# The first projection in two halves of 272 columns, copied unscaled, with idle transposes ahead: a two-block model on one core

## The chip, the core and the metric

The program runs on one core of one Trainium2 chip. The metric is the device time of one execution in microseconds, as the median of the runs. The core has five engines that each run their own list of instructions in order: TensorE (PE, matmuls; its weight loads are shown as PEld), VectorE (DVE), ScalarE (ACT), GpSimd (POOL) and SyncE (SP, which only issues DMA here).

## What is computed

Two blocks follow each other on 256 rows of 1024 numbers, in float32. The first block has a latent attention (MLA) and a differential attention side by side, a gated merge, and a mixture of 16 experts; the second has convolution, stick-breaking attention and gating, a feed-forward part and a gated projection. The change touches the very beginning, the latent attention's inputs:

```python
h = _rms_norm(x, attn_norm_w)
z = jnp.einsum('btd,dc->btc', h, w_in)
c_q, c_kv, k_rope, dq, dk, dv, g_mla, g_diff = _split_columns(z)      # 256, 256, 32, ...
q = jnp.einsum('btr,rc->btc', _rms_norm(c_q, mla_q_norm_w), mla_w_uq).reshape(b, t, 16, 96)
kv = jnp.einsum('btr,rc->btc', _rms_norm(c_kv, mla_kv_norm_w), mla_w_ukv).reshape(b, t, 16, 128)
k_nope, v_mla = kv[..., :64], kv[..., 64:]
```

The first 544 columns of `z` are `c_q`, `c_kv` and `k_rope`. The RMS norm of `x` multiplies each row by a factor (called rx below), and the norms of `c_q` and `c_kv` by two more (rc).

## The kernel before

The kernel is written on a scheduling layer. TensorE and GpSimd keep the order in which the code is written; ScalarE and VectorE are ordered by a static scheduler, except inside the block `with self.tc.manual_schedule(...)` of `mla` (L597 to L621), where they too keep the written order. DMA issues on SP are placed by the scheduler.

Products keep float32 accuracy by splitting each operand into a high and a low part: `mm3` (L207) issues three matmuls, high x high (L209), low x high (L210) and high x low (L211). A weight piece is split by `put` (L118): ScalarE casts the high part `wh` (L120), VectorE subtracts to get the low part `wl` (L121). `feed`, `take` and `look` (L123 to L139) hand the pieces out in order and split `ahead` + 1 of them early. Three pairs of `wh`, `wl` buffers go round; weight tiles arrive in a ring of four slots, and a slot is loaded again when its pieces are split. `transpose_split` (L147) transposes 128 columns of both row tiles on TensorE into one PSUM bank, ScalarE writes the high part and VectorE the low part of the scaled result.

The beginning of `mla` (L584) runs so. `x` arrives in two halves of 512 columns. TensorE transposes the four chunks of the first half, then of the second (L599, L603), into the banks `tr`, `o`, `tr`, `mm`. The 544 columns of `w_in` come as four tiles of two chunks of 128 rows each, 128 x 1088 numbers; `step` runs, for each of the eight chunks, the products into four banks (two row tiles, two column halves of 272), 96 in all. In between stand the tables of the rotary embedding (`tables`, L449): GpSimd computes the angles from the positions, ScalarE takes the sine (L483) and loads the table of the exponential (L484), GpSimd also fills the distances for the second attention (L480, L481). The row factor rx is made by `rms` on VectorE: squares (L535, L537) and then twelve small steps of an inverse root (`rsqrt`, L81). The four banks are copied to `cc` scaled by rx (`scaled`, L619), `cc` is transposed in four chunks (L626), the row factor rc of its two parts is made (L627 to L631), and `up` (L638) runs the second step: 36 products of 512 columns for q (L662, copied unscaled by `put_q`) and 48 for k and v (L692), whose results `put_kv` scales by rc on the way out of their banks: VectorE copies row tile 0, ScalarE row tile 1 (L659, L660). These groups of products take turns in three banks (`mm`, `mm`, `su`). The row sums of q's squares (L674, L675) are made meanwhile. The scratch tile `cn` for the squares of `cc` and the tile `di` of the distances share the memory `d1`.

After that come the remaining columns of `w_in`, the two attentions, the merge and the router. Then the expert weights, 403 MB, stream in from SP; their first slots come free as the pools of this front stage are closed.

Of the kernel before, what the change touches and what calls it, by code (L numbers as in the profile page):

```python
# [13 lines left out]
F32 = mybir.dt.float32  # L14
F32R = mybir.dt.float32r
I32 = mybir.dt.int32
# [58 lines left out]
class Kernel:  # L75
# [373 lines left out]
    def tables(self):  # L449
# [4 lines left out]
        pos_r = fp.tile([128, T], I32, name="pos_r")  # L454
        nc.sync.dma_start(pos_r, A["positions"].to_broadcast((128, T)))
# [20 lines left out]
        g.tensor_scalar(ang, ang, PI_IN, -PI_IN, op0=ALU.min, op1=ALU.max)  # L476
        di = fp.tile([128, NT, T], I32, name="di", tag="d1")
# [4 lines left out]
        yield  # L482
        nc.scalar.activation(rope, ang, AF.Sin)  # L483
        nc.scalar.activation(self.warm, self.warm, AF.Exp)  # L484
        yield
# [9 lines left out]
        for j in range(2):  # L495
            for i, (wi, si) in enumerate(((0, 1), (1, 0), (0, 0), (1, 1))):
                for t in range(NT):
                    g.tensor_tensor(
                        self.tab[:, j, i, t, :], rope[:, si, t, :], wr[:, j, 16 * wi : 16 * wi + 16], op=ALU.mult
                    )  # L500

    def lam(self):

        nc, A, fp, cp, c = self.nc, self.A, self.fp, self.cp, self.col
        lr = self.lr
# [15 lines left out]
        lp = fp.tile([128, 2, 64], F32, name="lp")  # L521
        ls = fp.tile([128, 2], F32, name="ls")
        nc.vector.tensor_tensor(lp, lr[:, 0::2, :], lr[:, 1::2, :], op=ALU.mult)
        nc.vector.tensor_reduce(ls, lp, axis=AX.X, op=ALU.add)
        nc.scalar.activation(ls, ls, AF.Exp)
        self.nlam = fp.tile([128, 1], F32, name="nlam")

        nc.vector.scalar_tensor_tensor(self.nlam, ls[:, 1:2], -0.2, ls[:, 0:1], op0=ALU.add, op1=ALU.subtract)
# [12 lines left out]
    def front_tiles(self):  # L541
# [4 lines left out]
        for k0 in (0, 2, 4, 6):  # L546
            yield self.wload(W[:, k0 : k0 + 2, 0:544], 2, 544)
# [36 lines left out]
    def mla(self, fb):  # L584
# [3 lines left out]
        put = lambda cs: self.transpose_split(self.x, self.col["attn_norm_w"], xh, xl, cs, ("tr", "o", "tr", "mm"))  # L588

        def step(k, wh, wl):  # L590
            for t in range(NT):
                ts = slice(t * 128, t * 128 + 128)
                for h in range(2):
                    hs = slice(272 * h, 272 * h + 272)
                    self.mm3(pss[t][h][:, :272], xh[:, k, ts], xl[:, k, ts], wh[:, hs], wl[:, hs], k == 0, k == 7)

        with self.tc.manual_schedule(engines={mybir.EngineType.Activation, mybir.EngineType.DVE}):  # L597
            next(self.const)
            put(range(4))  # L599
# [3 lines left out]
            put(range(4, 8))  # L603
            self.ahead = 1
            ws = []
            tables = self.tables()
            for k in range(8):
                ws = ws or self.take()
                step(k, *ws.pop(0))
                if k == 2:  # L610
                    next(tables)
                if k == 6:
                    next(tables)
                if k == 4:
                    self.rx = rx = self.rms(self.fa, self.x, self.od)
            cc = fb.tile([128, NT, 544], F32, name="cc", tag="d0")
            for h in range(2):
                for t in range(NT):
                    self.scaled(cc[:, t, 272 * h : 272 * h + 272], pss[t][h][:, :272], rx[:, t : t + 1], t == 0)  # L619
# [3 lines left out]
        cn = fb.tile([128, NT, 512], F32, name="cn", tag="d1")  # L623
        ch = fb.tile([128, 2, 4, T], F32R, name="ch", tag="d2")
        h, l = ch[:, 0], ch[:, 1]
# [1101 lines left out]
```

## Time and profile before

| | us |
|---|---|
| median of 3 runs (1518.96 to 1519.03) | 1519.02 |
| the profiled execution | 1517.97 |
| its span, from the first to the last event | 1516.3 |
| TensorE busy in the span | 1151.3 |
| VectorE busy | 478.4 |
| ScalarE busy | 356.8 |
| GpSimd busy | 133.2 |

Rows that are quoted below come from the profiled execution and are in microseconds from the start of its span. A timeline row names the start, the duration, the engine, the line of the kernel, the operation, the tile it writes and those it reads, its shape and how many were merged (x2); in brackets stands how long the engine was idle before it, and what ended that. Durations of neighbours overlap a little, since an engine starts an instruction before the last one's end is through. A stretch row gives the busy time of each engine between two moments, the number of instructions, and the TensorE clock that was granted as a share of the full one (1.00 is 2.4 GHz, 0.50 is 1.2 GHz); the column also prints 1.00 where no level was recorded, as in the first 14 us.

### The profile page before, as it was taken

What the parts mean: (1) busy time and instruction counts of PE and PEld (TensorE: products, weight loads), DVE (VectorE), ACT (ScalarE), POOL (GpSimd) and SP (SyncE); (2) the same over time, 40 slices, a digit from 0 to 9 for tenths busy, and PEclk for the clock granted to TensorE, in tenths of its full rate; (3) what the DMA queues carried; (4) which work ended last, traced back from release to release, by engine and by line L of the source; (5) the groups of instructions that cost most, each with busy time, mean ns of one, the idle gap of its engine ahead of it and who ended that gap; (6) DMA issues with size and microseconds to landing.
All of it is one profiled execution on the core that took longest, in us unless ns stands there. A gap on an engine that the chain in (4) does not pass through costs nothing.

```text
span 1516.3 us, 16564 instructions
## 1 busy us (share of the span) xinstructions
PE 1151.3 (76%) x6795; PEld 632.2 (42%) x6795; DVE 478.4 (32%) x969; ACT 356.8 (24%) x644; POOL 133.2 (9%) x181
## 2 busy tenths in 40 slices
PE   7999999895665586656566565656556899999998
PEld 6777896431111131111111111111111496889986
DVE  6987786410000000000000000000000576655456
ACT  5555565100000010000000000000000446544444
POOL 4613111000000000000000000000000034011010
PEclk9999999998778767787778877786787799999999
DMA  7633348999999999999999999999999862655530
GB/s 234 210 112 102 107 133 360 424 426 426 428 427 427 425 426 427 427 427 428 426 425 428 427 426 428 427 425 427 427 427 405 302 214 68 227 173 199 195 111 29
DMA packets 74826, 492.61 MB, mean 325 GB/s; under 512 B 5577, under 2 KB 9998, under 8 KB 50430
## 3 DMA queue, kind: packets, MB, share of 16 engines
q1 hardware_dynamic: 74350, 490.69, 80.0%
q8 instruction: 53, 0.87, 0.2%
q0 software_dynamic: 400, 0.86, 0.2%
q14 instruction: 23, 0.19, 0.0%
HBM read 490.48 MB, written 1.05 MB: 324 GB/s over the span
## 4 chain that ended last, share of the span: by engine, by line
DMA 49%; PE 39%; DVE 5%; issue 2%; ACT 2%; SPq 2%; POOL 1%; ACTq 0%; DVEq 0%; POOLq 0%
DMA w<-in_expert_w_down_dram 17%; DMA w<-in_expert_w_gate_dram 17%; DMA w<-in_expert_w_up_dram 14%; PE mm L209 5%; PE mm L210 5%; PE tr L1213 5%; PE mm L211 5%; PE acc L210 2%; PE acc L211 2%; PE acc L209 2%; PE su L1261 2%; DVE wl L121 1%; SPq L1280 1%; PE s L740 1%; PE o L1170 1%
## 5 line engine op out<-in xcount | busy, mean ns | idle before, releaser
L1213 PE MATMUL tr<-w,xe 128*32 128x512 f32 x2048 | 328.7, 775 | 196.8 <-DMA w<-in_expert_w_up_dram 112.5
L1213 PEld LDWEIGHTS tr<-w,xe 128*32 128x32 f32 x2048 | 65.2, 128 | 438.8 <-issue 168.0
L1261 PE MATMUL su<-w,hT 128*32 128x512 f32 x960 | 162.5, 815 | 93.9 <-DMA w<-in_expert_w_down_dram 85.2
L121 DVE TENSOR_TENSOR wl<-w,wh 128x1024 fp32r<-128x1024 f32 (+1 forms) x157 | 195.6, 1251 | 95.1 <-ACT wh L120 94.0
L120 ACT CAST wh<-w 128x1024 fp32r<-128x1024 f32 (+1 forms) x157 | 163.5, 1047 | 126.8 <-PE mm L211 54.0
L1239 DVE SCALAR_TENSOR_TENSOR hd<-tr,re,sg 128x512 f32<-128x512 f32 x16 | 12.0, 751 | 506.3 <-PE tr L1213 505.4
L1250 ACT ACTIVATE yh<-su,cols 128x512 fp32r<-128x512 f32 x17 | 11.7, 688 | 560.0 <-PE su L1261 524.6
L209 PE MATMUL mm<-xh,wh 128*128 128x256 f32 x448 | 128.4, 287 | 0.0
L211 PE MATMUL mm<-xl,wh 128*128 128x256 f32 x448 | 125.9, 281 | 0.0
L210 PE MATMUL mm<-xh,wl 128*128 128x256 f32 x448 | 125.8, 281 | 0.0
L1261 PEld LDWEIGHTS su<-w,hT 128*32 128x32 f32 x960 | 31.4, 132 | 208.4 <-DMA w<-in_expert_w_down_dram 133.3
L1251 DVE SCALAR_TENSOR_TENSOR yl<-su,cols,yh 128x512 fp32r<-128x512 f32 x17 | 12.8, 751 | 273.3 <-ACT yh L1250 273.3
L209 PEld LDWEIGHTS mm<-xh,wh 128*128 128x128 f32 x448 | 84.4, 188 | 2.8 <-issue 2.3
L210 PEld LDWEIGHTS mm<-xh,wl 128*128 128x128 f32 x448 | 84.5, 189 | 0.3
L211 PEld LDWEIGHTS mm<-xl,wh 128*128 128x128 f32 x448 | 84.4, 188 | 0.0
L1237 ACT ACTIVATE sg<-tr,re 128x512 f32<-128x512 f32 x16 | 11.0, 687 | 268.1 <-PE tr L1213 262.8
L209 PE MATMUL mm<-wh,xh 128*128 128x512 f32 (+1 forms) x144 | 59.8, 416 | 0.7 <-ACT xh L155 0.5
L1356 POOL TENSOR_SCALAR_AFFINE_SELECT m_gt<-ones 128x128 f32<-128x128 f32 x1 | 0.3, 289 | 648.2 <-PE tr L1213 648.2
L210 PE MATMUL mm<-wh,xl 128*128 128x512 f32 (+1 forms) x144 | 55.9, 388 | 1.0 <-DVE xl L156 1.0
L211 PE MATMUL mm<-wl,xh 128*128 128x512 f32 (+1 forms) x144 | 55.6, 386 | 0.0
L209 PE MATMUL acc<-wh,fhl 128*128 128x512 f32 x128 | 50.0, 391 | 0.0
L211 PE MATMUL acc<-wl,fhl 128*128 128x512 f32 x128 | 50.0, 390 | 0.0
(447 smaller groups left out, 1531.6 us busy)
## 6 DMA issues: line engine op xcount, KB each, us to landing
w<-in_expert_w_up_dram SPq DMA_DIRECT2D x64, 2048.0 KB
w<-in_expert_w_gate_dram SPq DMA_DIRECT2D x63, 2048.0 KB
w<-in_expert_w_down_dram SPq DMA_DIRECT2D x59, 2048.0 KB
w<-in_w_ff_dram SPq DMA_DIRECT2D x32, 1024.0 KB
w<-in_w_in_dram SPq DMA_DIRECT2D x29, 1024.0 KB
w<-in_expert_w_down_dram SPq DMA_DIRECT2D x10, 1024.0 KB
w<-in_w_out_dram SPq DMA_DIRECT2D x6, 1024.0 KB
w<-in_w_ple_gate_dram SPq DMA_DIRECT2D x4, 1024.0 KB
```

The lines of the kernel that those rows point to most:

```text
L120: self.nc.scalar.copy(h, src)
L121: (self.nc.gpsimd if pool else self.nc.vector).tensor_tensor(l, src, f(h), op=ALU.subtract)
L209: mm(out, ah, bh, start=start, stop=False, **kw)
L210: mm(out, al, bh, start=False, stop=False, **kw)
L211: mm(out, ah, bl, start=False, stop=stop, **kw)
L740: nc.tensor.matmul(S[:, t, :], qT[:, t * 128 : t * 128 + 128], kT, start=True, stop=True)
L1170: nc.tensor.matmul(ps, xk, self.oh[h][t], start=t == 0, stop=t == 1)
L1213: nc.tensor.matmul(ps[32 * j : 32 * j + 32, :], self.xe[k // 4][:, k % 4, 32 * e : 32 * e + 32], ws[k % 2][:, 0, 512 * j : 512 * j + 512], ...
L1239: nc.vector.scalar_tensor_tensor(hd, gu[1], re, sg, op0=ALU.mult, op1=ALU.mult)
L1251: nc.vector.scalar_tensor_tensor(yl, d, gate, f(yh), op0=ALU.mult, op1=ALU.subtract)
L1261: nc.tensor.matmul(d[r : r + 32, :], hT[:, a, j, :], ws[a // 2][:, a % 2, 512 * b : 512 * b + 512], start=j == 0 and a < 2, stop=j == 3 an ...
L1280: nc.sync.dma_start(w, A["expert_w_down"][0, 15, 512 * j : 512 * j + 512, bs].rearrange("(p a) n -> p a n", a=4))
```

## The change

The 544 columns are now done as two halves of 272, one after the other. Each weight tile holds four chunks of 128 rows of one half (128 x 4 x 272, again 128 x 1088 numbers, rows of 272 numbers instead of 544). The products of the first half and the first four chunks need one weight tile and the first half of `x`; only behind them does the code transpose the second half of `x`, into the banks `tr`, `o`, `tr`, `o`. Each half is copied to `cc` without the factor rx (`fetch`). The transposes of chunks 0 and 1 of `cc` stand between the two groups of products of the second half, those of chunks 2 and 3 behind the first 12 products of q. The factor is folded in later: the sums of squares under rc are multiplied by rx twice, rc by rx once, and GpSimd scales the 32 columns of `k_rope` by rx. Eight transposes of the identity into a bank that nobody reads (`busy`) stand ahead of the transpose of the first vectors, and eight behind it. The position load for the angles goes ahead of three of the weight tiles, the wide one and the distances go behind the sine, and the factor lambda of the second attention moves from `lam` to the end of `tables`. The other lines are as they were.

```diff
@@ tables
-        pos_r = fp.tile([128, T], I32, name="pos_r")
-        nc.sync.dma_start(pos_r, A["positions"].to_broadcast((128, T)))
...
-        di = fp.tile([128, NT, T], I32, name="di", tag="d1")
-        self.dist = fp.tile([128, NT, T], F32, name="dist")
-        for t in range(NT):
-            nc.gpsimd.tensor_tensor(di[:, t, :], pos_r, pos_c[:, t : t + 1].to_broadcast((128, T)), op=ALU.subtract)
-        nc.gpsimd.tensor_copy(self.dist, di)
         yield
         nc.scalar.activation(rope, ang, AF.Sin)
         nc.scalar.activation(self.warm, self.warm, AF.Exp)
         yield
+        pos_r = fp.tile([128, T], I32, name="pos_r")
...
+        nc.gpsimd.tensor_copy(self.dist, di)
         nc.scalar.activation(self.dist, self.dist, AF.Abs)
...
+        nc.vector.tensor_tensor(lp, lr[:, 0::2, :], lr[:, 1::2, :], op=ALU.mult)
+        nc.vector.tensor_reduce(ls, lp, axis=AX.X, op=ALU.add)
+        nc.scalar.activation(ls, ls, AF.Exp)
...
@@ front_tiles
-        for k0 in (0, 2, 4, 6):
-            yield self.wload(W[:, k0 : k0 + 2, 0:544], 2, 544)
+        for c0 in (0, 272):
+            for k0 in (0, 4):
+                yield self.wload(W[:, k0 : k0 + 4, c0 : c0 + 272], 4, 272)
@@ mla
+        def steps(h, ks, ws):
+            for k, (wh, wl) in zip(ks, ws):
+                for t in range(NT):
+                    ts = slice(t * 128, t * 128 + 128)
+                    self.mm3(pss[t][h][:, :272], xh[:, k, ts], xl[:, k, ts], wh, wl, k == 0, k == 7)
+
+        def fetch(h):
+            for t in range(NT):
+                (nc.vector.tensor_copy if t else nc.scalar.copy)(cc[:, t, 272 * h : 272 * h + 272], pss[t][h][:, :272])
...
+            tables = self.tables()
+            self.busy(8, "su")
             next(self.const)
+            next(tables)
+            self.busy(8, "su")
             put(range(4))
             pss = [[self.bank("s"), self.bank("mm")] for t in range(NT)]
             self.ahead = 0
             self.look()
-            put(range(4, 8))
+            steps(0, range(4), self.take())
+            put(range(4, 8), ("tr", "o"))
+            self.look()
...
+            self.sumsq(ss, self.x, self.od)
             self.ahead = 1
-            for k in range(8):
-                ws = ws or self.take()
-                step(k, *ws.pop(0))
...
+            steps(0, range(4, 8), self.take())
+            fetch(0)
+            steps(1, range(4), self.take())
+            self.transpose_split(cc, self.col["mla_q_norm_w"], h, l, range(2), ("tr", "o"))
+            ws = self.take()
+            next(tables)
+            self.rsqrt(rx, ss, 1.0 / D)
+            steps(1, range(4, 8), ws)
+            fetch(1)
+
+            for t in range(NT):
+                g.tensor_scalar(cc[:, t, 512:544], cc[:, t, 512:544], rx[:, t : t + 1], None, op0=ALU.mult)
...
-        up(0, 1536, put_q)
+        q_in = up(0, 1536, put_q)
+        next(q_in)
+        self.transpose_split(cc, self.col["mla_q_norm_w"], h, l, range(2, 4), ("tr", "o"))
...
+            nc.vector.tensor_scalar(sc[:, :, t], sc[:, :, t], r, r, op0=ALU.mult, op1=ALU.mult)
+        self.rsqrt(rc, sc, 1.0 / 256)
+        for t in range(NT):
+            nc.vector.tensor_scalar(rc[:, :, t], rc[:, :, t], rx[:, t : t + 1], None, op0=ALU.mult)
+        for _ in q_in:
+            pass
```

The order of the built programs shows three places where instructions moved. Numbers behind a name tell buffers apart. On ScalarE, between the first weight piece (`wh`) and the sine (`rope`), the order before is:

```order
L120 CAST wh_165<-w_105 128x1088
L155 ACTIVATE xh_108<-tr_169,vT_99 128x256
L155 ACTIVATE xh_108<-o_174,vT_99 128x256
L155 ACTIVATE xh_108<-tr_179,vT_99 128x256
L155 ACTIVATE xh_108<-mm_184,vT_99 128x256
L120 CAST wh_191<-w_189 128x1088
L120 CAST wh_221<-w_219 128x1088
L120 CAST wh_299<-w_297 128x1088
L535 ACTIVATE od_111,ss_315<-x_75 128x1024
L120 CAST wh_349<-w_347 128x1024
L483 ACTIVATE rope_262<-ang_260 128x64
L484 ACT_TABLE_LOAD
```

and now, from the first piece to the fourth:

```order
L120 CAST wh_227<-w_105 128x1088
L155 ACTIVATE xh_108<-tr_255,vT_99 128x256
L155 ACTIVATE xh_108<-o_260,vT_99 128x256
L155 ACTIVATE xh_108<-tr_265,vT_99 128x256
L155 ACTIVATE xh_108<-o_270,vT_99 128x256
L120 CAST wh_277<-w_275 128x1088
L535 ACTIVATE od_111,ss_281<-x_75 128x1024
L120 CAST wh_287<-w_285 128x1088
L600 COPY cc_136<-s_223 128x272
L120 CAST wh_319<-w_317 128x1088
```

The three pieces that stood together behind the conversions of the second half of `x` (`xh`) are now apart: one behind these conversions, one behind the squares, one behind the copy of the first half (`cc`). The sine and the table load come after them, at the end of the second half.

On VectorE, around the factor rc and the first scaled copies of k and v (`qk`, `v`), the order before is:

```order
L97 SCALAR_TENSOR_TENSOR rs_u_439<-rs_u_439,rs_a_436 128x4
L98 SCALAR_TENSOR_TENSOR rc_435<-rs_u_439,rs_y_438 128x4
L654 COPY qk_452<-mm_487 128x512
L121 TENSOR_TENSOR wl_467<-w_464,wh_466 128x1024
L121 TENSOR_TENSOR wl_503<-w_464,wh_502 128x1024
L654 COPY qk_452<-mm_507 128x512
L675 TENSOR_REDUCE ssq_540<-od_111 128x16
L205 TENSOR_SCALAR qk_452<-mm_588,rc_435 128x4x64
L121 TENSOR_TENSOR wl_581<-w_578,wh_580 128x1024
L205 TENSOR_SCALAR v_453<-mm_588,rc_435 128x256
```

and now:

```order
L696 TENSOR_REDUCE ssq_571<-od_111 128x16
L97 SCALAR_TENSOR_TENSOR rs_u_502<-rs_u_502,rs_a_499 128x4
L98 SCALAR_TENSOR_TENSOR rs_y_501<-rs_u_502,rs_y_501 128x4
L96 TENSOR_TENSOR rs_u_502<-rs_y_501 128x4
L97 SCALAR_TENSOR_TENSOR rs_u_502<-rs_u_502,rs_a_499 128x4
L98 SCALAR_TENSOR_TENSOR rc_496<-rs_u_502,rs_y_501 128x4
L681 TENSOR_SCALAR rc_496<-rc_496,rx_282 128x2 x2
L205 TENSOR_SCALAR qk_447<-mm_619,rc_496 128x4x64
L205 TENSOR_SCALAR v_448<-mm_619,rc_496 128x256
```

Before, rc stood ahead of both row sums of q (`ssq`); now its last steps and the two products by rx come behind both, and the first scaled copy right after them.

On TensorE the program begins before with:

```order
L413 MATMUL tr_138<-ident_89,vab_100 128x12
L153 MATMUL tr_141<-ident_89,x_75 128x128 x2
L153 MATMUL o_146<-ident_89,x_75 128x128 x2
L153 MATMUL tr_151<-ident_89,x_75 128x128 x2
L153 MATMUL mm_156<-ident_89,x_75 128x128 x2
L153 MATMUL tr_169<-ident_89,x_75 128x128 x2
L153 MATMUL o_174<-ident_89,x_75 128x128 x2
L153 MATMUL tr_179<-ident_89,x_75 128x128 x2
L153 MATMUL mm_184<-ident_89,x_75 128x128 x2
L209 MATMUL s_161<-wh_165,xh_108 128x272
L210 MATMUL s_161<-wh_165,xl_109 128x272
```

and now with:

```order
L186 MATMUL su_141<-ident_89 128x128 x8
L413 MATMUL tr_150<-ident_89,vab_100 128x12
L186 MATMUL su_194<-ident_89 128x128 x8
L153 MATMUL tr_203<-ident_89,x_75 128x128 x2
L153 MATMUL o_208<-ident_89,x_75 128x128 x2
L153 MATMUL tr_213<-ident_89,x_75 128x128 x2
L153 MATMUL mm_218<-ident_89,x_75 128x128 x2
L209 MATMUL s_223<-wh_227,xh_108 128x272
L210 MATMUL s_223<-wh_227,xl_109 128x272
L211 MATMUL s_223<-wl_228,xh_108 128x272
```

The idle transposes (`su`) stand around the one of the vectors (`vab`), and the transposes of the second half of `x` are gone from ahead of the first products.

## Rows read from the trace of the kernel before

**Rows 1.** Stretches: from:to, length, busy us (xinstructions) by engine, PEclk, DMA share, GB/s.

```profile
5.00:10.00 5.00, 2.63 (x13) 2.26 (x13) 3.06 (x6) 3.00 (x6) 0.00 (x0) 1.00 0.99 357
24.40:27.60 3.20, 0.34 (x2) 0.14 (x1) 3.19 (x7) 2.59 (x6) 3.20 (x8) 1.00 0.03 11
27.60:31.00 3.40, 3.16 (x11) 2.88 (x12) 3.37 (x15) 2.65 (x7) 2.81 (x14) 0.50 0.31 44
31.00:43.30 12.30, 11.94 (x51) 9.24 (x51) 10.66 (x21) 8.76 (x13) 5.62 (x7) 1.00 0.93 326
75.00:226.00 151.00, 147.99 (x971) 124.39 (x971) 123.02 (x322) 86.77 (x227) 30.05 (x16) 1.00 0.35 112
```

**Rows 2.** Chain of waits from 330 us: start, us, what.

```profile
340.46 32.49 DMA w<-in_expert_w_gate_dram
```

**Rows 3.** Timeline of SyncE's queue: start, us, line, what; the first expert load.

```profile
226.10 0.35 SPq L294 DMA_DIRECT2D w<-in_expert_w_gate_dram  x1
```

**Rows 4.** TensorE's timeline, 4 to 53 us: start, us, line, what, [idle before <-releaser].

```profile
4.72 0.69 PE L153 MATMUL tr<-ident,x 128*128 128x128 f32 x2
...
10.65 0.57 PE L209 MATMUL s<-wh,xh 128*128 128x272 f32 x1
...
14.10 0.29 PE L209 MATMUL mm<-wh,xh 128*128 128x272 f32 x1
...
24.13 0.29 PE L211 MATMUL mm<-wl,xh 128*128 128x272 f32 x1
...
27.84 0.47 PE L153 MATMUL tr<-ident,cc 128*128 128x128 f32 x1 [1.75 <-DVE cc L205]
...
29.24 0.78 PE L209 MATMUL mm<-wh,ch 128*128 128x512 f32 x1
...
31.07 0.39 PE L210 MATMUL mm<-wh,ch 128*128 128x512 f32 x1
...
42.54 0.40 PE L211 MATMUL mm<-wl,ch 128*128 128x512 f32 x1
43.31 0.47 PE L209 MATMUL mm<-wh,ch 128*128 128x512 f32 x1 [0.37 <-DVE v L205]
...
51.85 0.27 PE L413 MATMUL tr<-ident,vab 63*128 63x63 f32 x1
```

**Rows 5.** ScalarE's timeline, 5 to 25 us.

```profile
5.45 0.47 ACT L155 ACTIVATE xh<-tr,vT 128x256 fp32r<-128x256 f32 x1 [3.15 <-PE tr L153]
...
7.11 1.10 ACT L120 CAST wh<-w 128x1088 fp32r<-128x1088 f32 x1
...
22.79 1.28 ACT L484 ACT_TABLE_LOAD   x1
...
24.29 1.03 ACT L120 CAST wh<-w 128x1024 fp32r<-128x1024 f32 x1
```

**Rows 6.** VectorE's timeline, 8 to 40 us.

```profile
8.24 1.29 DVE L121 TENSOR_TENSOR wl<-w,wh 128x1088 fp32r<-128x1088 f32 x1 [0.52 <-ACT wh L120]
...
19.98 0.17 DVE L90 TENSOR_SCALAR rs_a<-ss 128x2 f32<-128x2 f32 x1
...
22.41 0.16 DVE L96 TENSOR_TENSOR rs_u<-rs_y 128x2 f32<-128x2 f32 x1
...
24.61 1.21 DVE L121 TENSOR_TENSOR wl<-w,wh 128x1024 fp32r<-128x1024 f32 x1
...
35.11 0.16 DVE L98 SCALAR_TENSOR_TENSOR rc<-rs_u,rs_y 128x4 f32<-128x4 f32 x1
...
38.83 0.68 DVE L654 COPY qk<-mm 128x512 f32<-128x512 f32 x1
39.49 1.75 DVE L675 TENSOR_REDUCE ssq<-od 128x16 f32<-128x1536 f32 x1
```

**Rows 7.** GpSimd's timeline around the table of distances.

```profile
22.45 1.17 POOL L480 TENSOR_TENSOR di<-pos_r,pos_c 128x256 int32<-128x256 int32 x2
23.69 0.62 POOL L481 CAST dist<-di 128x512 f32<-128x512 int32 x1
```

More of the change, by code (lines that the diff above doesn't have):

```diff
@@ L500, in tables @@
                     )
+        lr = self.lr
+        lp = fp.tile([128, 2, 64], F32, name="lp")
+        ls = fp.tile([128, 2], F32, name="ls")
+        nc.vector.tensor_tensor(lp, lr[:, 0::2, :], lr[:, 1::2, :], op=ALU.mult)
+        nc.vector.tensor_reduce(ls, lp, axis=AX.X, op=ALU.add)
+        nc.scalar.activation(ls, ls, AF.Exp)
+        self.nlam = fp.tile([128, 1], F32, name="nlam")
+        nc.vector.scalar_tensor_tensor(self.nlam, ls[:, 1:2], -0.2, ls[:, 0:1], op0=ALU.add, op1=ALU.subtract)
     def lam(self):
-        nc, A, fp, cp, c = self.nc, self.A, self.fp, self.cp, self.col
-        lr = self.lr
+        nc, A, cp, c = self.nc, self.A, self.cp, self.col
         self.rw = cp.tile([128, 8, 16], F32, name="rw")
@@ L520, in lam @@
         nc.gpsimd.tensor_copy(self.onr, self.ones[:16, :])
[L521 to L528, printed above, removed]
     def sumsq(self, dst, x, j, act=True):
@@ L586, in mla @@
         xh, xl = self.xh, self.xl
-        put = lambda cs: self.transpose_split(self.x, self.col["attn_norm_w"], xh, xl, cs, ("tr", "o", "tr", "mm"))
-        def step(k, wh, wl):
-            for t in range(NT):
[L592 to L595, printed above, removed]
+        put = lambda cs, tags=("tr", "o", "tr", "mm"): self.transpose_split(
+            self.x, self.col["attn_norm_w"], xh, xl, cs, tags)
+        def steps(h, ks, ws):
[4 more added lines that the diff above has]
+        def fetch(h):
+            for t in range(NT):
+                (nc.vector.tensor_copy if t else nc.scalar.copy)(cc[:, t, 272 * h : 272 * h + 272], pss[t][h][:, :272])
+        cc = fb.tile([128, NT, 544], F32, name="cc", tag="d0")
+        cn = fb.tile([128, NT, 512], F32, name="cn", tag="d1")
+        ch = fb.tile([128, 2, 4, T], F32R, name="ch", tag="d2")
+        h, l = ch[:, 0], ch[:, 1]
         with self.tc.manual_schedule(engines={mybir.EngineType.Activation, mybir.EngineType.DVE}):
+            tables = self.tables()
+            self.busy(8, "su")
             next(self.const)
+            next(tables)
+            self.busy(8, "su")
             put(range(4))
@@ L602, in mla @@
             self.look()
[L603 to L619 removed]
+            steps(0, range(4), self.take())
+            put(range(4, 8), ("tr", "o"))
+            self.look()
+            ss = self.sm.tile([128, NT], F32, name="ss", tag="ss")
+            self.rx = rx = self.fa.tile([128, NT], F32, name="rx", tag="rx")
+            self.sumsq(ss, self.x, self.od)
+            self.ahead = 1
+            steps(0, range(4, 8), self.take())
[9 more added lines that the diff above has]
+                g.tensor_scalar(cc[:, t, 512:544], cc[:, t, 512:544], rx[:, t : t + 1], None, op0=ALU.mult)
             for _ in tables:
@@ L651, in up @@
                         done(n0 + n, t, pss[t])
+                    yield
         def put_q(n, t, ps):
@@ L691, in mla @@
             g.tensor_tensor(q2, tm[2], tm[3], op=ALU.add)
-        up(2, 2048, put_kv)
+        for _ in up(2, 2048, put_kv):
+            pass
         next(self.const)
```

23 lines of the change are left out of this document (10 added, 13 removed).

## The prediction

> **What bounds the kernel now.** I read the stretches first, then the chain of waits, then the engines one by one over the first 52 us. From 340 us the chain is one expert-weight transfer after another [rows 2], so there only the moment at which that stream starts can move the end; its first load is issued at 226.10 us [rows 3], and what lets it go is the front stage that ends then. The front stage is TensorE's: 148.0 of 151 us from 75 to 226 us [rows 1]. Nothing in it is tied to a clock time, so a shift of TensorE at 52 us should reach the end whole. What the change touches lies before that. There TensorE runs 96 products of 272 columns from 10.65 to 24.4 us, stands almost idle to 27.84, transposes the result and starts the second step at 29.24 us; that step has 84 products of 512 columns (36 for q, 48 for k and v) and ends at the transpose of 51.85 us [rows 4]. The reader is to see that the hole of TensorE is no hole of the other two: in 24.4 to 27.6 us DVE is busy for 3.19 of 3.20 us and ACT for 2.59 [rows 1].
>
> **Prices.** 272-column products come every 0.23 us at first (15 from 10.65 to 14.10) and every 0.125 us later (80 from 14.10 to 24.13); 512-column ones every 0.234 us (49 from 31.07 to 42.54); a transpose takes 0.20 us at the lower of the two clock levels (seven from 27.84 to 29.24), so about 0.11 at the upper [rows 4]. Four conversions of transposed x take 0.42 us each on ACT (5.45 to 7.11), a weight piece 1.10 us on ACT and then 1.29 us on DVE, the smaller ones 1.03 and 1.21 [rows 5, 6].
>
> **Start of the change.** The first eight idle transposes end before the vector load that releases the 4.55 us transpose; they cost nothing. The second eight stand between that transpose and those of x, whose half is there at 4.72: 8 x 0.20 = 1.6 us later. ACT then converts x and after it the first piece: ready at 7.11 + 1.10 + 1.6 = 9.8 us; DVE's low part at 8.24 + 1.29 + 1.6 = 11.1 us. The first group of 24 products starts two products early and then waits for that low part; 22 remain. At the lower level throughout they end at 11.1 + 22 x 0.23 = 16.2 us; at the upper throughout at 13.9; if the clock rises where it does now (14.0 us) at 15.2. I take 15.2 and call that moment E, with 13.9 and 16.2 as ends. What the rows say on the idle transposes: x's transposes from 4.72 us on did not raise the clock for the products at 10.65 us, and 24.4 to 27.84 us of near idleness brought the granted clock to 0.50, out of which transposes and products together lifted it by 31.07 us [rows 1, 4]. The Trainium skill, "TensorE: Matmul & The Clock Gate", Part 4, says that transposes don't count as TensorE activity in the way matmuls do; by that the eight and eight bring nothing and E lies between 15.2 and 16.2, against 13.9 if they count. The trace fits either.
>
> Landing: the tiles of 272 columns have the same 128 x 1088 numbers (557 KB) in rows of half the length. At the 357 GB/s of 5 to 10 us [rows 1] one takes 1.6 us (an estimate); twice as slow, the first would be there at 7.1 + 1.6 = 8.7 us, when ACT reaches it. The others are wanted later than now. Nothing.
>
> **From E to the second step.** Before, x's second half was transposed ahead of the first product, in time lost anyway. Now it stands behind the first 24, and ACT must convert it before it may touch the second piece (the order of ACT, shown with the change): conversions from E+0.5 to E+2.8 (the fourth waits 0.6 us for a single bank), the piece to E+3.9, DVE's low part to E+5.2. TensorE has 0.9 us of transposes in these 5.2. Then 22 products to E+8.0, 24 to E+11.0 and, behind four transposes, 24 to E+14.4: their pieces are ready in time, since ACT and DVE take 1.10 and 1.29 us a piece against 3.0 us of products. With E = 15.2 the second step begins at 29.6 us. The hole is closed, and nothing is won: 29.24 before.
>
> Then ACT has two conversions, a piece (to E+13.3), the sine, the table load of 1.28 us [rows 5] and the second copy of the result (to E+15.4) ahead of the next piece, ready E+16.35; DVE has eleven small steps of the root (0.22 us each: 19.98 to 22.41 [rows 6]) ahead of its low part, ready E+17.85. TensorE gets three products, waits, and ends the first twelve at E+17.85 + 7 x 0.234 = E+19.5; four transposes and 24 products more make E+25.6. Those 36 q products ended at 31.07 + 32 x 0.234 = 38.6 us before (the fifth starts at 31.07 [rows 4]); now 40.8, 2.2 us late.
>
> **Where most of it comes from.** The factor rc scales the k and v results out of their banks, and there are three banks. Before it was ready at 35.11 us, ahead of both row sums of q (39.49 is the first) [rows 6], and the first k/v group waits for a bank only 0.37 us, at 43.31 [rows 4]. Now the squares under its root can't begin until POOL has converted the distances, because the scratch tile of the squares shares memory with them: rx and the last copy are there at E+18.4, two scalings by rx take some 0.6 us on POOL (an estimate), the differences 1.17 and the conversion 0.62 [rows 7], E+20.8; lambda, ahead on DVE, waits for ACT behind the absolute value, E+21.7. And in DVE's order both row sums of q stand ahead of rc's last steps. DVE from E+21.7, with the rows' times less the 0.08 us by which one instruction starts before the last one's end: squares, low parts and small steps to E+23.9, a copy of 0.6 us, two pieces (ACT delivers at 24.65 and 25.6) to 27.1, a copy, a row sum of 1.67 to 29.5, a piece and a row sum to 32.9, five root steps and two products to 34.2, two scaled copies to E+35.1 [rows 6]. TensorE has filled three banks by E+30.1: three groups of six products from 25.6, plus 0.3 us for a low part. It waits 5.0 us. The shorter gap of before lowered the clock for 3.2 us of work (27.84 to 31.07, products every 0.46 us [rows 4]); that is seven products here, 1.6 us, of which 0.5 fall into the next wait, so 1.1. 30 products (7.0 us) and 0.7 us for the low part of the last piece (E+38.3) then end at E+43.9. Sum: E + 43.9 - 51.85 = E - 7.95, so **+7.2 us** at E = 15.2, +5.9 at 13.9, +8.2 at 16.2. The unscaled copies themselves, the moved lambda, the two products by rx on the 4-column sums and the position load are below 1 us of DVE and are in that list. DVE's list has some 25 entries; I allow 1 us either way.
>
> The profiled execution took 1517.97 us (span 1516.3), 1.05 us under the median of the runs, 1519.02. So 1525.2 on its footing, **1526.2 us** as a median.
>
> **Rivals.** *Faster:* TensorE alone is the bound and every piece is ready when it asks. Then E = 13.9, 72 products at 0.125, 16 transposes at 0.11 and 84 products at 0.234 end at 13.9 + 9.0 + 1.8 + 19.7 = 44.4 us, 7.4 us early: 1511.6. For it: the 3.4 us hole and the slow products after it are real [rows 1, 4]. Against: DVE's busy 3.19 of 3.20 us in just that hole. It decides by whether the low part of the second piece is there at E+0.9 rather than E+5.2, and rc by E+30. 14%.
> *No change to speak of:* rc is not late, because DVE gets through its list some 5 us sooner than I add up. TensorE then runs on from E+30.1: 7.0 + 0.7 us, to E+37.8, so 1.2 us late at E = 15.2 and level at 13.9: 1518.9 to 1520.2. For it: before, DVE is idle for 1.6 us in 31 to 43.3 us [rows 1]; against: no more than that, and five are wanted. This takes in that the later stages give part of the delay back. 18%.
> *Slower through the clock:* the idle transposes don't lift it and the slow stretch lasts to E = 16.2; +8.2, 1527.2. This is the skill's rule at its hardest. 20%.
> The forecast itself, with E from 13.9 to 15.2: 48%.
>
> **Numbers.** Less than 0.2% (3 us) can't be told from no change here. Slower: 48 + 20 = 68%; within: 18%; faster: 14%. The range must hold 8 in 10: it leaves out the faster rival and a little above the slowest one: 1516.0 to 1529.0; the likeliest case's own is 1524 to 1528.
>
> **What would show it.** Right: TensorE's second group of 24 starts some 5 us after the first ends, behind ACT's casts; the second step starts within 1 us of 29.2 us; TensorE waits several us in the k/v products for DVE's scaled copy; the 51.85 us transpose comes at about 59; the first expert load is issued some 7 us after 226. Wrong: rc ready before the k/v products, a second step that starts before 27 us, or products at 0.125 us from the first one on.

## The result and the profile after

The changed kernel takes 1534.45 us (median of 4 runs, 1532.88 to 1534.64) against 1519.03 for the kernel before on the same chip: a ratio of 1.0096, 95% interval 1.0084 to 1.0108. It is 15.4 us slower, where 7.2 were forecast: the sign was right, the size was half of what came, and the time lies 5.4 us above the range's upper end of 1529.0. The profiled execution took 1534.35 us with a span of 1532.6, so 16.3 us more of span than before.

The shift is complete when the front's first two steps are over, and passes on almost unchanged. The transpose of the constants, 51.85 us in [rows 4], comes at 67.89 us (+16.04), and the first expert load, 226.10 us in [rows 3], leaves at 242.70 (+16.6):

```profile
242.70 0.35 SPq L294 DMA_DIRECT2D w<-in_expert_w_gate_dram  x1
```

The stretches of the changed kernel, to be laid beside [rows 1] (length, busy time and instructions of TensorE, its weight loads, VectorE, ScalarE and GpSimd, TensorE's granted clock, share of the DMA engines, GB/s):

```profile
10.00:14.00 4.00, 2.75 (x14) 2.53 (x15) 1.29 (x1) 0.39 (x1) 3.55 (x17) 0.82 1.09 293
14.00:24.40 10.40, 7.30 (x35) 6.51 (x34) 5.38 (x8) 4.70 (x8) 2.90 (x9) 0.66 0.51 159
24.40:27.60 3.20, 3.20 (x21) 3.20 (x20) 0.57 (x2) 1.39 (x2) 0.00 (x0) 0.71 0.85 264
31.00:43.30 12.30, 10.64 (x47) 8.36 (x47) 9.58 (x34) 8.61 (x20) 6.97 (x22) 0.86 0.93 320
43.30:52.10 8.80, 6.52 (x28) 4.90 (x26) 8.80 (x14) 5.58 (x6) 8.80 (x17) 1.00 0.40 128
52.10:75.00 22.90, 16.85 (x61) 13.19 (x62) 17.81 (x34) 11.13 (x16) 10.97 (x23) 0.78 0.32 96
75.00:226.00 151.00, 147.35 (x912) 122.06 (x911) 123.61 (x317) 82.61 (x201) 31.34 (x17) 1.00 0.37 119
```

The old hole of 24.4 to 27.6 us is closed (TensorE busy 3.20 of 3.20 us, 0.34 before). In its place stand an idle stretch in 14 to 24.4 us, a granted clock of 0.66 in it and of 0.71 in the next row, and a second hole that ends behind 52.1 us, with a granted clock of 0.78 in that row. VectorE and GpSimd are both busy for all of 43.3 to 52.1. TensorE's timeline of the same kernel (start, duration, line, what, [idle before <-releaser]) shows where these lie:

```profile
10.44 0.40 PE L209 MATMUL s<-wh,xh 128*128 128x272 f32 x1 [1.55 <-ACT wh L120]
...
11.77 0.40 PE L211 MATMUL s<-wl,xh 128*128 128x272 f32 x1 [0.81 <-DVE wl L121]
12.00 0.29 PE L209 MATMUL s<-wh,xh 128*128 128x272 f32 x1
12.13 0.29 PE L210 MATMUL s<-wh,xl 128*128 128x272 f32 x1
...
12.67 0.43 PE L211 MATMUL s<-wl,xh 128*128 128x272 f32 x1
12.89 0.43 PE L209 MATMUL s<-wh,xh 128*128 128x272 f32 x1
...
16.04 0.29 PE L211 MATMUL s<-wl,xh 128*128 128x272 f32 x1
...
21.34 0.59 PE L211 MATMUL s<-wl,xh 128*128 128x272 f32 x1 [0.51 <-DVE wl L121]
...
26.25 0.29 PE L211 MATMUL s<-wl,xh 128*128 128x272 f32 x1
...
58.15 0.80 PE L209 MATMUL mm<-wh,ch 128*128 128x512 f32 x1 [8.33 <-ACT v L203]
58.74 0.63 PE L210 MATMUL mm<-wh,ch 128*128 128x512 f32 x1
...
67.89 0.27 PE L413 MATMUL tr<-ident,vab 63*128 63x63 f32 x1
```

The first group of 24 starts at the upper level (0.125 us from 12.00 on), falls to the lower one at 12.67 (0.227 us) and ends at 16.17, the moment E. The second group runs at 0.227 us from 21.34 almost to its end, 26.38. The second step starts at 32.83 us, and in it TensorE waits 8.33 us for the scaled copies; 12 products at 0.43 us follow.

Two numbers carry everything below: **S**, the start of the second step, and **R**, from S to the transpose behind the k/v products. Before: S = 29.24, R = 22.61. After: S = 32.83 (+3.6), R = 35.06 (+12.4). Forecast: S = 29.6, R = 29.5.

What fills R is seen on VectorE (the four-column steps are rc's root, L121 a weight's low part, L696 a row sum of q, L205 the scaled copy):

```profile
49.15 1.84 DVE L121 TENSOR_TENSOR wl<-w,wh 128x1024 fp32r<-128x1024 f32 x1
50.91 0.68 DVE L98 SCALAR_TENSOR_TENSOR rs_y<-rs_u,rs_y 128x4 f32<-128x4 f32 x1
...
51.87 1.74 DVE L696 TENSOR_REDUCE ssq<-od 128x16 f32<-128x1536 f32 x1
53.53 0.51 DVE L97 SCALAR_TENSOR_TENSOR rs_u<-rs_u,rs_a 128x4 f32<-128x4 f32 x1
54.07 0.65 DVE L98 SCALAR_TENSOR_TENSOR rs_y<-rs_u,rs_y 128x4 f32<-128x4 f32 x1
...
56.12 0.65 DVE L98 SCALAR_TENSOR_TENSOR rc<-rs_u,rs_y 128x4 f32<-128x4 f32 x1
...
57.14 0.48 DVE L205 TENSOR_SCALAR qk<-mm,rc 128x256 f32<-128x256 f32 x1
```

and beside it on GpSimd (q's rotary multiplications):

```profile
49.86 1.71 POOL L712 TENSOR_TENSOR qk<-tm 128x256 f32<-128x256 f32 x1
...
52.61 2.77 POOL L710 TENSOR_TENSOR tm<-qk,tab 128x256 f32<-128x256 f32 x4
55.35 0.71 POOL L711 TENSOR_TENSOR qk<-tm 128x256 f32<-128x256 f32 x1
56.03 0.71 POOL L712 TENSOR_TENSOR qk<-tm 128x256 f32<-128x256 f32 x1
```

The order is the one forecast: both row sums ahead of rc's last steps. The durations are not: the steps that took 0.16 us in [rows 6] take 0.51 to 0.68 in these rows.

A second, smaller difference stands ahead of rc's squares. GpSimd's two scalings of `k_rope` by rx take 1.75 us, and VectorE's list waits behind them for lambda (`nlam`), as the prediction has it:

```profile
36.27 1.75 POOL L635 TENSOR_SCALAR cc<-cc,rx 128x32 f32<-128x32 f32 x2 [18.69 <-DVE rx L98]
```

```profile
40.62 0.16 DVE L509 SCALAR_TENSOR_TENSOR nlam<-ls 128x1 f32<-128x1 f32 x1 [0.78 <-ACT ls L506]
```

### The profile page after: what moved, and what is told of

Its sections match the earlier page's. It is cut to its first block, busy times and chain, and to the rows that moved or that the text cites. A ratio compares the mean times of both kernels' runs of the same rounds, so it can differ in the third digit from the quotient of the medians.

```text
span 1532.6 us, 16595 instructions
## 1 busy us (share of the span) xinstructions
PE 1141.4 (74%) x6811; PEld 632.1 (41%) x6811; DVE 481.1 (31%) x973; ACT 356.2 (23%) x644; POOL 127.2 (8%) x183
## 3 DMA queue, kind: packets, MB, share of 16 engines
HBM read 490.48 MB, written 1.05 MB: 321 GB/s over the span
## 4 chain that ended last, share of the span: by engine, by line
DMA 49%; PE 39%; DVE 6%; ACT 2%; issue 2%; SPq 2%; POOL 1%; ACTq 0%; DVEq 0%; POOLq 0%
DMA w<-in_expert_w_down_dram 18%; DMA w<-in_expert_w_gate_dram 16%; DMA w<-in_expert_w_up_dram 14%; PE mm L209 5%; PE mm L210 5%; PE tr L1235 5%; PE mm L211 5%; PE acc L211 2%; PE acc L210 2%; PE acc L209 2%; PE su L1283 2%; DVE wl L121 2%; SPq L1302 1%; PE s L762 1%; PE s L211 1%
## 5 line engine op out<-in xcount | busy, mean ns | idle before, releaser
L1235 PE MATMUL tr<-w,xe 128*32 128x512 f32 x2048 | 319.9, 756 | 213.0 <-DMA w<-in_expert_w_up_dram 125.7
L121 DVE TENSOR_TENSOR wl<-w,wh 128x1024 fp32r<-128x1024 f32 (+1 forms) x157 | 196.0, 1252 | 95.2 <-ACT wh L120 93.9
L1272 ACT ACTIVATE yh<-su,cols 128x512 fp32r<-128x512 f32 x17 | 11.7, 687 | 566.6 <-PE su L1283 533.2
```

The source lines that it names most:

```text
L121: (self.nc.gpsimd if pool else self.nc.vector).tensor_tensor(l, src, f(h), op=ALU.subtract)
L1235: nc.tensor.matmul(ps[32 * j : 32 * j + 32, :], self.xe[k // 4][:, k % 4, 32 * e : 32 * e + 32], ws[k % 2][:, 0, 512 * j : 512 * j + 512], ...
L1272: nc.scalar.activation(yh, d, AF.Identity, scale=gate)
```

## The experiments

All are edits of the changed kernel, in the order of the argument. The table has S and R, the longest wait for the scaled copies in the k/v products, the transpose that ends R, and the time against the kernel before on the same chip:

| run | S | longest wait | R | transpose | time minus before |
|---|---|---|---|---|---|
| before | 29.24 | 0.37 | 22.61 | 51.85 | |
| changed kernel | 32.83 | 8.33 | 35.06 | 67.89 | +15.4 |
| e1 no idle transposes | 31.95 | 8.36 | 35.09 | 67.04 | +14.4 |
| e2 x first | 23.59 | 7.91 | 34.30 | 57.89 | +7.8 |
| e10 x first, no idle transposes | 25.43 | 7.84 | 34.73 | 60.16 | +6.6 (one run) |
| e11 hole filled | 30.41 | 8.65 | 34.32 | 64.73 | +12.3 (one run) |
| e3 rotary behind k/v in the code | 34.05 | 8.33 | 35.23 | 69.28 | +16.1 |
| e5 rotary behind rc | 33.65 | 4.21 | 30.07 | 63.72 | +11.3 (one run) |
| e4 rc inside the squares | 33.72 | 2.99 | 30.92 | 64.64 | +11.4 |
| e6 own scratch | 32.39 | 7.25 | 33.21 | 65.60 | +12.2 (one run) |
| e12 = e11 + e5 | 30.19 | 4.59 | 30.35 | 60.54 | +9.7 |
| e7 three parts | 23.44 | 1.05 | 31.58 | 55.02 | -0.7 |
| e8 six parts | 23.84 | 1.06 | 25.90 | 49.74 | -3.2 |
| e9 six parts, x's scratch | 24.87 | 1.04 | 25.76 | 50.63 | -1.7 |

**The start: idle transposes and the order of x.**

```diff
 e1
-            self.busy(8, "su")
             next(self.const)
             next(tables)
-            self.busy(8, "su")
             put(range(4))
```

> The changed kernel without its two groups of eight idle transposes; the rest as it is. In the changed kernel the first product starts at 10.44 us and the first ones come every 0.125 us, then every 0.227 us from 12.67 to 15.84. Theory A, the idle transposes lifted the clock: without them x's transposes start 1.7 us earlier, the first product at 8.7 us, but the products come every 0.23 us from the first one on; the first 24 end near 15.0 us instead of 16.17, and the whole is 1.0 to 1.5 us shorter (1533). Theory B, they do nothing for the clock: the first products come every 0.125 us without them too, the first 24 end near 14.4 us, 1.7 us shorter. Rival: without them the clock stays low into the second group and the 1.7 us are lost again (1534.5).

Without them every product of the first group is slow, as theory A has it (TensorE's timeline; 21 products 0.227 us apart from 10.50 to 15.03):

```profile
10.50 0.43 PE L209 MATMUL s<-wh,xh 128*128 128x272 f32 x1
...
15.03 0.35 PE L211 MATMUL s<-wl,xh 128*128 128x272 f32 x1
```

The group ends at 15.2, 1.0 us sooner than with them, S comes 0.9 us sooner and R is the same: here they cost about 1 us more than they save. The time (1.0092, 1.0075 to 1.0109) can't be told from the changed kernel's.

```diff
 e2
+            put(range(4, 8))
             steps(0, range(4), self.take())
-            put(range(4, 8), ("tr", "o"))
```

> The changed kernel with one part undone: the second half of x is transposed ahead of the first 24 products, as in the kernel before. If the second group of products starts 5.2 us after the first (20.0 and 21.3 us against 16.17) because ACT and DVE convert x's second half and the second piece only then, it now starts right behind the first group, ends 5 to 7 us earlier (26.37 us now), the second step starts at 26 to 28 us (32.83 now), the factors of k and v come as much earlier, and the time is 5 to 7 us shorter, 1528. Rival: the factors hang on GpSimd's chain (positions, angles, distances), which doesn't move; then the wait in the k and v products grows from 8.3 us by what the start wins, and the time stays at 1534.

The first theory, in full: S is 9.2 us earlier and the time 1.0051 times the kernel before (1.0034 to 1.0068), 7.6 us less than with the change whole. More is won than the 5 to 7 us expected, because the clock stays up too: 68 products in a row, from 11.50 us on, come at 0.125 us. R hardly moves, so the wait is not GpSimd's angles, whose clock time would have stayed:

```profile
48.50 0.77 PE L209 MATMUL mm<-wh,ch 128*128 128x512 f32 x1 [7.91 <-DVE v L205]
```

The run e10 takes both edits.

> The run with x's second half first, without the two groups of idle transposes: with the run without them alone, the one with x first alone and the changed kernel this completes a square of two parts. If the idle transposes only lift the clock for the first 24 products, these come every 0.23 us here, begin 1.2 us earlier and end near 15.1 us instead of 14.0; the second half of the products is at 0.125 us and the end is 0 to 1 us later than with x first alone (1527 to 1528). Rival: without them the clock stays low to the second group, and it is 3 to 4 us later; or the earlier start wins and it is 1 us earlier (1526).

Products 0.227 us apart up to 15.19, 0.125 behind. S is 1.8 us later than in e2, 0.4 of it from the vector load ahead of the first transpose (4.98 against 4.54 us); yet the one time, 6.6 us over the kernel before, is not later than e2's 7.8. A single time can't decide a microsecond: what the idle transposes are worth with x first lies between nothing and 1.4 us.

```diff
 e11
             put(range(4, 8), ("tr", "o"))
+            self.busy(12, "tr")
```

> The changed kernel with twelve more idle transposes in the hole of TensorE between the transposes of x's second half and the second group of 24 products (18.7 to 20.0 us). Theory: the second group comes every 0.227 us instead of 0.125 because TensorE stood still before it; with the hole filled it comes at 0.125 us, ends near 24.2 us instead of 26.37, and all behind it follows: 2 us shorter than the changed kernel, 1532.4. Rival: the clock is low there whatever TensorE does in the hole; then the twelve only delay, 0 to 1 us longer.

Twelve idle transposes in the hole, and the second group comes at 0.125 us:

```profile
18.04 1.47 PE L186 MATMUL tr<-ident 128*128 128x128 f32 x12
...
21.32 0.29 PE L209 MATMUL s<-wh,xh 128*128 128x272 f32 x1
21.44 0.29 PE L210 MATMUL s<-wh,xl 128*128 128x272 f32 x1
...
23.83 0.29 PE L211 MATMUL s<-wl,xh 128*128 128x272 f32 x1
```

From E (15.9) to S are 14.5 us; the forecast has 14.4, the changed kernel 16.7. So the forecast missed S by the clock of the second group and by E, and by nothing else. The wait grows by 0.3 us; 3.2 us are left at the transpose.

**The wait.** The first try missed its aim.

```diff
 e3
-        <the loop of q's rotary multiplications>
         for _ in up(2, 2048, put_kv):
             pass
+        <the loop of q's rotary multiplications>
```

> The changed kernel with GpSimd's rotary multiplications of q written behind the k/v products; VectorE's own order is the same, row for row. Theory 1: the four-column steps of the root take 0.65 us instead of 0.18 because GpSimd runs beside them. Then they take 0.2 us here, the low part of 1.84 us takes 1.22 again, the factor is ready at 53.4 us instead of 57.1, TensorE waits 4.6 us instead of 8.3, and the time is 3.5 to 4.5 us shorter, 1530.5. Theory 2: they are slow for a reason of their own (their chain of results): 0.65 us again, 1534.4. Rival: q's rotary part is then late for the scores, and the 4 us are lost again behind 68 us.

Nothing moved in R, and neither theory is tested: GpSimd has no instruction in the k/v products, so the later place in the code is the same place in its queue. Its multiplications still run from 47.59 to 57.96, as here:

```profile
53.82 2.78 POOL L712 TENSOR_TENSOR tm<-qk,tab 128x256 f32<-128x256 f32 x4
```

A true dependence does it:

```diff
 e5
+        g.tensor_copy(self.sm.tile([128, 2, NT], F32, name="rcc", tag="rcc"), rc)
         <the loop of q's rotary multiplications>
```

> The changed kernel with one added instruction: GpSimd copies the factor rc into a scratch tile ahead of q's rotary multiplications, so that they can't run before rc is there; VectorE's and ScalarE's order is the same, row for row. Theory, GpSimd's multiplications beside them slow VectorE's four-column steps: they take 0.16 to 0.2 us instead of 0.5 to 0.68, the low part behind them 1.22 instead of 1.84 us; seven steps and one low part, 3.5 us sooner: TensorE waits 4.8 us instead of 8.3 and the end comes 3.5 to 4.5 us earlier, near 1530.5. Rival, they are slow by their own chain of results: 0.65 us again, the end where it was, 1534.5. Rival, q's rotary part comes too late for the scores behind 75 us: the steps are short and the end is where it was.

VectorE's list in the same order, without GpSimd beside it:

```profile
49.28 1.21 DVE L121 TENSOR_TENSOR wl<-w,wh 128x1024 fp32r<-128x1024 f32 x1
50.42 0.15 DVE L98 SCALAR_TENSOR_TENSOR rs_y<-rs_u,rs_y 128x4 f32<-128x4 f32 x1
...
53.29 0.16 DVE L98 SCALAR_TENSOR_TENSOR rc<-rs_u,rs_y 128x4 f32<-128x4 f32 x1
```

and on TensorE:

```profile
54.84 0.79 PE L209 MATMUL mm<-wh,ch 128*128 128x512 f32 x1 [4.21 <-ACT v L203]
```

Steps of 0.15 to 0.16 us, a low part of 1.21: the theory. From S to the restart of TensorE are 21.2 us; the forecast has 20.7 (50.3 minus 29.6), the changed kernel 25.3. One GpSimd loop is 4.1 us of the wait. (The run was taken once; the step durations and the wait are rows of its trace.)

```diff
 e4
-            nc.scalar.activation(j, q[:, t], AF.Square)
+            nc.scalar.activation(j, q[:, t], AF.Square, scale=rc[:, 0, t : t + 1])
...
-        for t in range(NT):
-            r = rc[:, 0, t : t + 1]
-            nc.vector.tensor_scalar(sq[:, t, :], sq[:, t, :], r, r, op0=ALU.mult, op1=ALU.mult)
```

> The changed kernel with the factor of q applied inside the squares of q (the scale of ACT's square) instead of behind them: both row sums of q, and GpSimd's rotary multiplications that wait for the squares, can only come behind the factors' root. Theory (order and GpSimd together): the factor is ready some 7 us earlier, 3.7 for the slowed steps and 3.3 for the two row sums of 1.74 us, at 50 us; TensorE waits about 1 us instead of 8.3, doesn't cool down, the 51.85 us transpose of the kernel before comes at 58 to 59 us instead of 67.9, the time is 8 to 9 us shorter, 1525.5 to 1526.5. If GpSimd isn't the cause of the slow steps: 3.3 us shorter, 1531. Rival: the squares and sums, now between the k/v copies, delay those copies, and the gain is half.

The wait falls by 5.3 us, and 1.9 come back as two further waits, since q's squares and row sums now stand among the copies: the rival, "the gain is half"; 4.0 us against the changed kernel where 8 to 9 were expected. This run also holds the cleanest pair of rows. GpSimd multiplies q to 51.11 us (47.25 + 3.86), and VectorE's steps change at that moment:

```profile
47.25 3.86 POOL L710 TENSOR_TENSOR tm<-qk,tab 128x256 f32<-128x256 f32 x4
```

```profile
47.93 1.21 DVE L121 TENSOR_TENSOR wl<-w,wh 128x1024 fp32r<-128x1024 f32 x1
...
50.43 0.70 DVE L98 SCALAR_TENSOR_TENSOR rs_y<-rs_u,rs_y 128x4 f32<-128x4 f32 x1
51.17 0.16 DVE L96 TENSOR_TENSOR rs_u<-rs_y 128x4 f32<-128x4 f32 x1
```

Here the low part keeps its 1.21 us, and it is GpSimd's four multiplications that take 3.86 us instead of 2.77: which of the two engines stands differs.

```diff
 e6
-        cn = fb.tile([128, NT, 512], F32, name="cn", tag="d1")
+        cn = fb.tile([128, NT, 512], F32, name="cn")
```

> The changed kernel with memory of its own for the scratch tile of the squares under rc, which no longer waits for GpSimd's distances. By the prediction's step (the squares can't begin until the distances are converted, lambda behind them) rc moves by what they waited, from 40.6 us to about 37.5, 2 to 3 us: TensorE waits 5 to 6 us instead of 8.3, 1531.5. Rival: VectorE's list between 43 and 57 us, with both row sums of q and the steps that GpSimd slows, sets rc by itself: below 1 us of gain, 1534.

From S to TensorE's restart at 57.03 us are 24.6 us instead of 25.3: the shared scratch was worth 0.7 us, not the 2 to 3 expected. The edit frees only half of the chain, though. VectorE's list still waits for lambda, which comes behind the distances, and reaches its squares 7.8 us behind S in both kernels:

```profile
40.19 0.16 DVE L509 SCALAR_TENSOR_TENSOR nlam<-ls 128x1 f32<-128x1 f32 x1 [0.89 <-ACT ls L506]
```

What lambda's wait is worth was not tried; VectorE is idle for 0.89 us there, so hardly more than that. That VectorE's list decides the rest is likely, but not shown by this run. R is 1.85 us shorter; the other 1.2 lie behind the restart, where 6 products come at the lower level instead of 12. The one time, 3.2 us nearer to the kernel before than the changed kernel's, looks like the expected gain and isn't evidence for it: 0.4 us of it is an earlier S, 1.2 the clock behind the restart.

**Both terms together.**

> The changed kernel with the two additions together that moved it apart: twelve idle transposes in the hole ahead of the second group, and GpSimd's rotary multiplications behind rc. If the prediction's sum failed in these two terms alone (the second group at the lower clock, the root's steps slowed by GpSimd), the k/v products now end where it put them, E + 43.9 = 60 us with E at 16, instead of 67.9: the transpose of the constants at 60 to 61 us, TensorE's wait in the k/v products near 5 us, the time 7.5 to 9.5 us longer than the kernel before. Rival, the two overlap (an earlier second step only lengthens the wait, as it did with the twelve transposes alone, 8.7 us): 63 to 64 us, 11 to 12 us longer.

```profile
51.38 0.80 PE L209 MATMUL mm<-wh,ch 128*128 128x512 f32 x1 [4.59 <-ACT v L203]
...
60.54 0.27 PE L413 MATMUL tr<-ident,vab 63*128 63x63 f32 x1
```

The forecast's clock times, with E at 15.7: S 30.1 (measured 30.19), the wait 5.0 (4.59), the transpose 59.6 (60.54, and not the rival's 63 to 64). So the two terms add up. The ratio is 1.0066 (1.0049 to 1.0083). At 9.7 us the time lies just past the 7.5 to 9.5 expected: 8.7 us at the transpose have become 10.8 at the first expert load (236.90 us). Part of that is in the trace: behind the transpose TensorE waits 0.76 us for a low part, which the kernel before doesn't, and 1.5 instead of 1.0 for the k of the scores.

**What the change is worth when repaired.** e7 is e2 + e4 + e6; e8 adds e5, takes rx's root ahead of the low parts of the first two result chunks, and the sine behind the second copy:

```diff
 e8, beside e2, e4, e5 and e6
             steps(1, range(4), self.take())
+            self.rsqrt(rx, ss, 1.0 / D)
             self.transpose_split(cc, self.col["mla_q_norm_w"], h, l, range(2), ("tr", "o"))
             ws = self.take()
-            next(tables)
-            self.rsqrt(rx, ss, 1.0 / D)
             steps(1, range(4, 8), ws)
             fetch(1)
+            next(tables)
```

> The changed kernel with x's second half transposed ahead of the first products, a scratch tile of its own for the squares under rc, and rc inside q's squares, so that the row sums stand behind the root. From the run with x first alone: TensorE has filled its three banks at 40.6 us and then waits 7.9 us. With rc ready by 38 us it doesn't wait there, doesn't cool down, and the k/v products end near 48.5 us (51.85 before the change): 3 us shorter than the kernel before, 1516. Rival: the row sums now stand between the k/v copies, as in the run with rc inside the squares, where a second wait of 1.6 us came from them: 1517.5 to 1519. Rival: GpSimd still slows the root; rc at 41 to 42 us: 1518.

> The same three parts and three more: rx's root ahead of the low parts of the first two result chunks on VectorE, the sine with its table load behind the second copy of the result on ScalarE, and GpSimd's rotary multiplications behind rc. In the run with x first alone the second step waits 0.82 and 0.83 us for weights behind the table load and the root; these go, and the root of rc runs at 0.2 us a step: the k/v products end at 45 to 47.5 us, 4.5 to 7 us ahead of the kernel before, 1512 to 1514.5. Rival: what starts earlier waits later (scores, diff weights) and the end is that of the run with three parts.

e7 is level with the kernel before (1.0001, 0.9991 to 1.0010), where 3 us less were expected: its k/v products end at 55.0 us instead of 48.5, with no one long wait, but with TensorE held for 0.4 to 1.8 us at a time by copies, low parts and row sums on VectorE, and with 12 products 0.43 us apart behind the first three of these waits. e8 is 0.19% faster than the kernel before (0.9981, 0.9971 to 0.9991), less than expected too. Its S of 23.84 is 5.4 us ahead of the kernel before, and R gives 3.3 of it back. The three waits below come to 2.7 us. The first ends with the first scaled copies behind rc; the others with copies that stand behind a square of q on ScalarE and a row sum on VectorE.

```profile
40.27 0.47 PE L209 MATMUL mm<-wh,ch 128*128 128x512 f32 x1 [0.97 <-DVE v L205]
...
42.53 0.50 PE L209 MATMUL mm<-wh,ch 128*128 128x512 f32 x1 [0.63 <-ACT v L203]
...
48.17 0.47 PE L209 MATMUL mm<-wh,ch 128*128 128x512 f32 x1 [1.06 <-DVE v L205]
```

```profile
39.23 1.58 ACT L695 ACTIVATE od<-qk,rc 128x1536 f32<-128x1536 f32 x1 [3.74 <-DVE rc L681]
```

```profile
44.75 1.74 DVE L696 TENSOR_REDUCE ssq<-od 128x16 f32<-128x1536 f32 x1
```

```diff
 e9, against e8
-        cn = fb.tile([128, NT, 512], F32, name="cn")
...
-            self.sumsq(sc[:, i, :], cc[:, :, 256 * i : 256 * i + 256], cn[:, :, 256 * i : 256 * i + 256])
+            self.sumsq(sc[:, i, :], cc[:, :, 256 * i : 256 * i + 256], self.od[:, :, 256 * i : 256 * i + 256])
```

> The run with six parts, but the squares under rc go into the scratch of x's squares, which nobody reads, instead of new memory. In the run with six parts the k/v products ended 2.1 us ahead of the kernel before (49.74 against 51.85 us), the first expert load left 6 us ahead but the ones from 252 us on only 1.0 us: the new tile moves the rings of the later stages in memory. Theory: without new memory the load order of the kernel before comes back, the first expert load at 224 us, and the whole 2.1 us arrive: 2 us shorter than the kernel before. Rival: the end depends on when the last front products end and not on the order of loads: as with new memory, 1 to 1.5 us shorter in the profiled runs.

The load order of the kernel before did come back, with the first expert load at 226.43 us, but the gain didn't grow to the 2 us expected: 0.999 (0.9981 to 0.9999), 1.7 us by the medians. This profiled execution began at the lower clock (S 1.0 us later than e8), and the scores then wait 1.9 us (1.0 before). How much of the transpose's lead arrives at the end, and whether the new tile helps or hurts it, stays open.

## Why the prediction fell short

- **Right:** TensorE is the front's bound and its shift reaches the end (16.04 us at the transpose, 16.3 in the span). The second group waits on ScalarE's and VectorE's conversions; closing the old hole wins nothing in this order; rc comes behind both row sums, TensorE fills three banks and waits several us for the scaled copy. The chain of causes was the one forecast; the sizes of four of its terms were not.
- **The first failed step: "then 22 products to E+8.0".** The second group was priced at 0.125 us. It took 0.227 and ended at E + 10.2; S came 2.2 us later for it (e11). The prediction lowered the clock after its 5.0 us wait but not after the 5.2 us between E and the second group, though [rows 1, 4] showed 3.4 us of near idleness do just that.
- **The second: rc's "small steps", priced with a row of [rows 6].** Those stand where GpSimd does not multiply beside them. In their new place GpSimd turns q, and the steps and one low part take 4.1 us more (e5, e4). This is the largest term. Another 0.5 us of the later rc lies ahead of the squares: the two scalings on GpSimd were put at 0.6 us, a figure that no row of before shows, and took 1.75 us; lambda comes 7.8 us behind S instead of 7.3.
- **E was 16.17, not 15.2** (+1.0). Some 0.6 us of it came before the clock mattered: the first low part was there at 11.7 us instead of 11.1, since the transpose of the first vectors came at 5.04 us (4.55 before) and the second eight idle ones took 1.76 us instead of 1.6. The other 0.3 is the clock. So this was the 20% rival's E, but not by its reason: the first products came at the upper level, and it fell again at 12.67 us, after TensorE had stood for 1.55 and 0.81 us.

```profile
10.42 1.29 DVE L121 TENSOR_TENSOR wl<-w,wh 128x1088 fp32r<-128x1088 f32 x1 [0.50 <-ACT wh L120]
```

- **The slow stretch after the wait** was mis-sized: the first 13 products took 2.6 us more than at 0.234 us, where 1.1 were priced. The 0.7 us priced for the last low part didn't come, so some 1.0 more of R is left. Sum: 2.2 (the second group) + 4.6 (rc, of which GpSimd's slowing 4.1) + 1.0 (E) + 1.0 = 8.8 us, which is 67.89 minus the 59.1 forecast.
- **A cause that was named and weighs little:** the scratch shared with the distances, 0.7 us (e6), with lambda's wait left in place.
- **The rivals:** rc was late, so "no change" failed at its condition. "Faster" needed the second piece's low part at E + 0.9; e2 gives just that by the old order of x, and its S of 23.6 is 5.6 us early, but rc still cost it the rest.

## What to carry to other kernels

A duration belongs to the place where it was read: before moving an instruction, look at what else runs at the new place, and price small VectorE steps beside a busy GpSimd at up to four times their idle cost. A stall of TensorE costs its length and then the slow clock behind it: in all nine runs here with a wait of 4.2 us or more, 6 to 13 products behind it came at the slow spacing. Ask it of every stall in the sum, not only of the longest. To keep an engine's work away from a critical list, give it a true dependence; a later line in the code moves nothing if its queue holds nothing in between.

## What the runs showed of the hardware

**VectorE and GpSimd hold each other up.** A 128x4 step on VectorE takes 0.15 to 0.16 us alone and mostly 0.50 to 0.70 beside GpSimd's 128x256 multiplications (0.71 each); a low part 1.84 instead of 1.21; GpSimd's L712 1.71 instead of 0.71 while that low part runs. In e4 the low part is not slowed, and GpSimd is. A row sum (1.74, 1.75 in [rows 6]) and a copy out of a bank (0.68 in both) are not slowed. The Trainium skill, "Trainium Architecture — The Big Picture", section "What this means for kernel authors", says that this pair of engines shares a port pair under an exclusive lock, not a split of bandwidth. The trace is in line with that: a four-column step that reads almost nothing still takes 0.65 us, about as long as one GpSimd multiplication.

**Idle transposes seem to lift the clock, not in every execution.** With them the first product took 0.37 to 0.40 us in 7 of 11 profiled executions of the kernels here, the upper level, and 0.57 to 0.60 in 4 (e3, e4, e5, e9); without them (before, e1, e10) 0.57 to 0.59 in 3 of 3. Twelve in a hole kept the next group at the upper level both times (e11, e12); in the six kernels with the same hole and no transposes in it (the changed one, e1, e3, e4, e5, e6) that group came 0.227 us apart. The Trainium skill, "TensorE: Matmul & The Clock Gate", Part 4, says that transposes don't count as TensorE activity the way matmuls do; in these runs the products behind them mostly came at the upper level, so far as so few executions can say. Whether a group began at the upper level moves S by up to 1.2 us from run to run (32.83 and 34.05 in two kernels whose TensorE lists are alike).

**The spacing of equal products tells the level at the start.** In e1 the granted clock reads 1.00 for 10 to 14 us, where products come every 0.227 us.
